# Products over 64 channels run over all 128 partitions, with zeros in the other half

## The chip, the cores and the metric

The kernel runs on one core of one Trainium2 chip. Times are device microseconds of one execution; the metric is their median over runs. The profile is that of one execution. PE is TensorE's matmul, PEld its weight load, DVE is VectorE, ACT is ScalarE, POOL is GpSimd and SP is SyncE, whose queue issues most of the DMAs.

## What is computed

Two transformer blocks on 512 tokens with 1024 features, all in float32. The first block has two groups of heads side by side, then a dense feed-forward part. The second has retention heads and differential attention heads, then a layer that picks neurons out of 16384 by product keys. The change touches the scores of three of these groups, all of them sums over 64 channels:

```python
# recurrent heads (mLSTM): q, k have 64 channels per head
jnp.einsum('bhctd,bhcsd->bhcts', qc, kc)
# latent heads: 128 channels without and 64 with rotary positions
k = jnp.concatenate([k_nope, k_pe], axis=-1)        # 128 + 64
s = jnp.einsum('bhqd,bhkd->bhqk', q_blk, kh) * scale
# differential heads: two score maps p per head, 64 channels each
s = jnp.einsum('bhpid,bhpjd->bhpij', qi, kt) + bias
```

## The kernel before

**Precision.** Most products are split in two parts. A float32 value x is kept as `hi`, a copy in the format fp32r, and `lo`, the rest x - hi. A product is then the sum of three fp32r matmuls (`mm3`, L130 to L132): hi by hi, hi by lo, lo by hi. Matmuls on plain float32 tiles are done by the hardware in two instructions each.

**Scores over 64 channels.** For the recurrent and the differential heads the three parts are packed. The first tile of a head has hi in one half of the 128 partitions and lo (or hi once more) in the other, so that one matmul over 128 partitions does two of the three parts. The third part, with the lo half alone, is a matmul over 64 partitions: L652 and L653 in `rec_weights` (tile pS), L837 and L838 in `dif_scores` (tile pDS). Which half of the partitions it uses goes with the head or with the map (`up` is partitions 0 to 63, `dn_` 64 to 127). For the latent heads (tile psc), L556 is the product over the 128 plain channels, and L557 the one over the 64 rotary channels; two heads lie in the two halves of qT1 and kT1.

**Stages.** The first block's input product gives the gates (F7), the latent inputs (ch, cl), the features of the recurrent heads (qk, ql, from tile pq and a convolution) and rows for v and the output gate (tile pts, `ts_mm`). From the gates a chain of scans makes UB (L394 to L398), which is transposed in four pieces (L543, tile pub) into the columns `cols` and `em`; the recurrent heads use them. `lat_in`, `lat_norm` and `lat_heads` make qT0, kT0, qT1 and kT1 per block of 128 tokens. The latent attention then runs over 16 pairs of a head and a block of queries, staged: scores of one pair, transposes (tile ppt, L572) of the pair before, product with v (tile pov, L582) of the one before that. The recurrent heads are staged alike: scores and weights (`rec_weights`, DVE's L664 and L668, ACT's L665 and L667), three steps later `rec_out` (tile pH). The differential heads too: `dif_scores`, `dif_turn` (pDT), `dif_out` (pD), with the features of later heads (tile pf) and products for later stages (pts) in between.

**What sets the order.** Each engine works through its own queue in order. The order in each queue is fixed when the program is compiled: a planner goes through the program by priority and by the costs that it expects, so that work of later stages (products pq, pts, pf) is placed in the gaps of earlier ones. Tiles live in pools; a tile with a tag and `bufs=n` shares n places, and the first write to a place waits until its former owner has been read for the last time. A pool that is opened where others have been closed waits in the same way. PSUM has eight banks, four of them ("att") for the tiles of the attention stages and four ("acc") for the longer sums.

Of the kernel before, what the change touches and what calls it, by code (L numbers as in the profile page):

```python
# [7 lines left out]
F32 = mybir.dt.float32  # L8
# [9 lines left out]
T = 512  # L18
D = 1024
P = 128  # L20
# [30 lines left out]
def body(ctx, tc, I, out):  # L51
# [17 lines left out]
    def bank(tag, name):  # L69
        p, n = banks[tag]  # L70
        return p.tile([P, 512], F32, tag=tag, name=name, bufs=n)
# [9 lines left out]
    V.memset(nhalf, -0.5)  # L81

    up, dn_ = slice(0, 64), slice(64, 128)

    def sub(eng, o, a, hi):
        eng.tensor_tensor(o, a, hi.bitcast(F32), op=OP.subtract)  # L86
# [157 lines left out]
    def out_last(x, w, h, l, spare, after):  # L244
        pg = []
        for half in range(2):
            for j in range(2):
                if half * j:
                    raw = fetch(w[4 * half + j])
                    for kk in range(2):  # L250
                        ph, pl = spare(), spare()
                        c = slice(kk * 512, (kk + 1) * 512)
                        S.activation(ph, raw[:, c], AF.Copy)
                        sub(V, pl, raw[:, c], ph)
                        pg.append((ph, pl))
                else:
                    wh, wl = page(w[4 * half + j])
                    pg += [(wh[:, kk * 512:(kk + 1) * 512], wl[:, kk * 512:(kk + 1) * 512]) for kk in range(2)]
        for tb in range(NT):
            t = slice(tb * P, (tb + 1) * P)  # L260
            for half in range(2):
                c = slice(half * 512, (half + 1) * 512)
                ps = bank("acc", "pol")
                for kt in range(4):
                    wh, wl = pg[4 * half + kt]
                    mm3(ps, h[:, kt, t], l[:, kt, t], wh, wl, kt == 0, kt == 3)
                V.tensor_tensor(x[tb][:, c], x[tb][:, c], ps, op=OP.add)
            after(tb)

# [47 lines left out]
    nc.sync.dma_start(gcq, I["g_c"])  # L317
    gq_b = bcast_row(I["g_q"], 192, "gq_b", m1)
    gk_b = bcast_row(I["g_k"], 192, "gk_b", m1)
    gm_b = bcast_row(I["g_mlstm_out"], 512, "gm_b", m1)  # L320
    sin = m1.tile([P, NT, 32], F32, name="sin")
    cos = m1.tile([P, NT, 32], F32, name="cos")
    kpe = m1.tile([P, NT, 4, 16], F32, name="kpe")
# [66 lines left out]
    Mx = F7[0:64]  # L390
    V.tensor_tensor_scan(Bc[0:4], zf[0:4], zero[0:4], 0.0, op0=OP.add, op1=OP.add)
    V.tensor_tensor_scan(Bc[32:36, ::-1], zf[32:36, ::-1], zero[32:36], 0.0, op0=OP.add, op1=OP.add)
    UB = mc.tile([P, T], F32, name="UB")
    G.memset(UB, 0.0)  # L394
    V.tensor_tensor(UB[0:R], F7[0:R], Bc, op=OP.subtract)
    V.tensor_tensor_scan(Mx[0:4], UB[0:4], UB[0:4], 0.0, op0=OP.max, op1=OP.max)
# [4 lines left out]
    sub(V, MxP[64:128], Mx, MxP[0:64])  # L401
    for d in range(2):
        V.tensor_tensor(sel[:, d], ident[:, 32 * d:32 * d + 4], ident[:, 64 + 32 * d:68 + 32 * d], op=OP.add)


    lp, lp_close = pool("latp")
# [30 lines left out]
    ukv = page(I["w_ukv"][0], into=hk)  # L437
    qT0 = [main.tile([P, 2, T], F32, tag="x", name="qT0", bufs=NT) for _ in range(2)]
    kT0 = [main.tile([P, 2, T], F32, tag="x", name="kT0", bufs=NT) for _ in range(2)]
    qT1 = mb.tile([P, 2, T], F32, name="qT1")  # L440
    kT1 = mb.tile([P, 2, T], F32, name="kT1")
    vv = mb.tile([P, NT, 512], F32, name="vv")

# [15 lines left out]
    for tb in range(NT):  # L459
        sq = lp.tile([P, 192], F32, tag="qsq", name="psq", bufs=1)  # L460
        S.activation(sq[:, 0:64], kflat[:, tb], AF.Square, accum_out=ssp[:, tb:tb + 1])
    kg = lp.tile([P, NT, 64], F32, name="kg")
    V.tensor_tensor(kg, kflat, gk_b[:, None, 128:192].to_broadcast([P, NT, 64]), op=OP.mult)
    kr = lp.tile([P, NT, 64], F32, name="kr")
    rope(kr, kg, cos, sin)
# [58 lines left out]

    def lat_heads(tb, key):
        nope, rot = lat[tb, key]
        T0, T1 = (kT0, kT1) if key else (qT0, qT1)
        t = slice(tb * P, (tb + 1) * P)
        pt = bank("att", "pqt")
        for hd in range(4):  # L530
            PE.transpose(pt[:, hd * P:(hd + 1) * P], nope[:, hd, :], ident)
        for j in range(2):
            S.activation(T0[j][:, :, t], pt[:, j * 256:(j + 1) * 256].rearrange("p (h t) -> p h t", h=2), AF.Copy)
        pt = bank("att", "pqt")
        for j in range(2):
            PE.transpose(pt[:, j * P:(j + 1) * P], rot[:, 2 * j:2 * j + 2, :].rearrange("p h d -> p (h d)"), ident)
        S.activation(T1[:, :, t], pt[:, 0:256].rearrange("p (h t) -> p h t", h=2), AF.Copy)

    staged([(tb, key) for tb in range(NT) for key in range(2)], lat_in, lat_norm, lat_heads)

    pt = bank("att", "pub")
    for tb in range(NT):
        PE.transpose(pt[:, tb * P:(tb + 1) * P], UB[:, tb * P:(tb + 1) * P], ident)  # L543
    S.activation(cols, pt.rearrange("p (t a b c) -> p t a b c", t=NT, a=2, b=2)[:, :, :, :, 0:4], AF.Copy)
    Ucol = cols[:, :, 0]
    S.activation(em, cols[:, :, 1], AF.Exp, scale=-1.0)

    ybh, ybl = [m1.tile([P, 4, T], F32R, tag="yb", name="yb", bufs=2) for _ in range(2)]
    att = {}

    def lat_scores(hd, qb):
        pp = slice(64 * (hd % 2), 64 * (hd % 2) + 64)
        j, jj = hd // 2, hd % 2
        q = slice(qb * P, (qb + 1) * P)
        ps = bank("att", "psc")
        PE.matmul(ps, qT0[j][:, jj, q], kT0[j][:, jj, :], start=True, stop=False)  # L556
        PE.matmul(ps, qT1[pp, j, q], kT1[pp, j, :], start=False, stop=True)  # L557
        mx = small(1, "mx")
        V.tensor_reduce(mx, ps, axis=AX.X, op=OP.max)
        V.tensor_scalar(mx, mx, rq[:, qb, hd:hd + 1], -1.0, op0=OP.mult, op1=OP.mult)  # L560
        pe_ = mb.tile([P, T], F32, tag="pe", name="pe", bufs=3)
        sm = small(1, "sm")
        S.activation(pe_, ps, AF.Exp, bias=mx, scale=rq[:, qb, hd:hd + 1], accum_out=sm)
        V.reciprocal(sm, sm)
        V.tensor_scalar(pe_, pe_, sm, None, op0=OP.mult)
        att[hd, qb] = pe_
# [25 lines left out]
    for i in range(4):  # L592
        ps = bank("acc", "pq")
        ws_mm(ps, page(wf[i]), h, l)
        cv = mc.tile([P, T], F32, tag="cv", name="cv", bufs=2)
        V.tensor_scalar(cv, ps, convw[:, i, 2:3], convw[:, i, 5:6], op0=OP.mult, op1=OP.add)
        for j in (0, 1, 3, 4):
            a, b = max(0, 2 - j), min(T, T + 2 - j)
            V.scalar_tensor_tensor(cv[:, a:b], ps[:, a + j - 2:b + j - 2], convw[:, i, j:j + 1], cv[:, a:b],
                                   op0=OP.mult, op1=OP.add)  # L600
        th = mc.tile([P, T], F32, tag="th", name="th", bufs=1)
        S.activation(th, cv, AF.Tanh, scale=0.5)
        V.scalar_tensor_tensor(th, th, 1.0, cv, op0=OP.add, op1=OP.mult)
        if i < 2:
            ql = mv.tile([P, T], F32R, name=f"ql{i}")
        for m, (own, other) in enumerate(((up, dn_), (dn_, up))):
            a = mv.tile([P, T], F32R, name=f"qk{i}{m}")
            S.activation(a[own], th[own], AF.Copy)
            if i < 2:
                S.activation(a[other], th[own], AF.Copy)  # L610
                sub(V, ql[own], th[own], a[own])
                qk.append((a, ql))
            else:
                sub(V, a[other], th[own], a[own])
                qk.append(a)
# [16 lines left out]

    ma, ma_close = pool("rec")
    og = ma.tile([P, NT, 512], F32, name="og")
    rec = {}

    def rec_max(hd):
# [7 lines left out]
    def rec_weights(hd, sb):  # L645
        if sb == 0:
            rec_max(hd)
        pp = (up, dn_)[hd % 2]
        (qh, ql), kk = qk[hd], qk[4 + hd]
        sps = bank("att", "pS")  # L650
        t = slice(sb * P, (sb + 1) * P)
        PE.matmul(sps, kk[:, t], qh, start=True, stop=False)  # L652
        PE.matmul(sps, kk[pp, t], ql[pp], start=False, stop=True)  # L653
        for d in range(2):
            mp = rec[hd][d]
            uc = Ucol[:, sb, d, hd:hd + 1]
# [40 lines left out]
    for tb in range(NT):  # L697
        load_x(x, tb)
    out_half(x, I["w_out"], ybh, ybl, range(4), 2)
    yh, yl = [ma.tile([P, 4, T], F32R, name=n) for n in ("yh", "yl")]  # L700
    for hd in range(4):
        hs, hss = rec[hd, "o"]
        rh = small(4, "rh")
# [3 lines left out]
        for tb in range(NT):  # L707
            V.scalar_tensor_tensor(ya[:, tb], hs[:, tb], rh[:, tb:tb + 1], og[:, tb, hd * 128:(hd + 1) * 128],
                                   op0=OP.mult, op1=OP.mult)
            PE.transpose(pt[:, tb * P:(tb + 1) * P], ya[:, tb], ident)  # L710
        S.activation(yh[:, hd, :], pt, AF.Copy)
        sub(V, yl[:, hd, :], pt, yh[:, hd, :])
    h, l, _, norm, norm_end = norm_T(x, "g_ffn_norm")
    out_last(x, I["w_out"], yh, yl, lambda: ma.tile([P, T], F32R, tag=f"E{T}", name="X", bufs=4), norm)
    ma_close()
# [84 lines left out]

    def dif_key(hd, ps):
        B = [md.tile([P, T], F32R, tag=f"dk{m}", name="dk", bufs=2) for m in range(2)]
        kl = md.tile([P, T], F32R, tag="dkl", name="dkl", bufs=2)
        for m, (own, other) in enumerate(((up, dn_), (dn_, up))):
            S.activation(B[m][own], ps[own], AF.Copy)
            S.activation(B[m][other], ps[own], AF.Copy)
            sub(V, kl[own], ps[own], B[m][own])
        feat["k", hd] = B, kl

    def dif_head(hd):  # L810
# [16 lines left out]
    def dif_scores(hd, qb):  # L827
# [4 lines left out]
        w = max(n, 256)  # L832
        (B, kl), A = feat["k", hd], feat["q", hd]
        es, sms = [], []
        for m, pp in enumerate((up, dn_)):
            ps = bank("att", "pDS")
            PE.matmul(ps[:, 0:w], A[m][:, q], B[m][:, 0:w], start=True, stop=False)  # L837
            PE.matmul(ps[:, 0:w], A[m][pp, q], kl[pp, 0:w], start=False, stop=True)  # L838
            e = md.tile([P, T], F32, tag="sv", name="sv", bufs=5)
            V.scalar_tensor_tensor(e[:, 0:n], tri[:, T - n:T], float(2.0 ** (-8.0 * (hd + 1) / 4)), ps[:, 0:n],  # L840
                                   op0=OP.mult, op1=OP.add)
# [116 lines left out]

    staged([(hd, b) for hd in range(4) for b in range(NT)], ret_weights, skip, skip, skip, ret_out, *[skip] * 4, ret_norm)
    h, l, rows, norm, norm_end = norm_T(x, "norm_ffn_g")  # L960
    out_last(x, I["w_out2"], yh, yl, lambda: ma.tile([P, T], F32R, tag="X", name="X", bufs=4), norm)
    xn3 = rows[3]
    ma_close()
    mr_close()
# [477 lines left out]
```

## Time and profile before

| | |
|---|---|
| median of 3 runs | 2127.32 us (2127.05 to 2130.56) |
| profiled execution | 2128.51 us, span of its instructions 2126.7 us |
| mean granted TensorE clock | 0.995 |
| PE busy | 2090.7 us, 98% of the span |
| DVE busy | 1541.3 us, 72% |
| ACT busy | 858.6 us, 40% |
| POOL busy | 534.6 us, 25% |
| latent scores, first to last | 116 to 170 us |
| recurrent scores | 175 to 218 us |
| differential scores | 666 to 794 us |

The first row is what the change is timed by. The durations of single instructions come from the profiled execution, whose own time is the second row; its span runs from the first to the last instruction. Busy times of PE are of pipelined matmuls: the time between the starts of two neighbours says more than the length of one.

### The profile page before, as it was taken

What the parts mean: (1) busy time and instruction counts of PE and PEld (TensorE: products, weight loads), DVE (VectorE), ACT (ScalarE), POOL (GpSimd) and SP (SyncE); (2) the same over time, 40 slices, a digit from 0 to 9 for tenths busy, and PEclk for the clock granted to TensorE, in tenths of its full rate; (3) what the DMA queues carried; (4) which work ended last, traced back from release to release, by engine and by line L of the source; (5) the groups of instructions that cost most, each with busy time, mean ns of one, the idle gap of its engine ahead of it and who ended that gap; (6) DMA issues with size and microseconds to landing.
All of it is one profiled execution on the core that took longest, in us unless ns stands there. A gap on an engine that the chain in (4) does not pass through costs nothing.

```text
span 2126.7 us, 29751 instructions
## 1 busy us (share of the span) xinstructions
PE 2090.7 (98%) x10985; PEld 1807.7 (85%) x10985; DVE 1541.3 (72%) x3039; ACT 858.6 (40%) x1505; POOL 534.6 (25%) x387
## 2 busy tenths in 40 slices
PE   7999999999999999999999999999999999999998
PEld 6856888888888778888999999999888889899886
DVE  6846666556444763679979799978888878778784
ACT  5645354444324543311335544333333333333332
POOL 1100034444100000100000004544555554444330
PEclk9999999999999999999999999999999999999999
DMA  5210269899512222354898778999999999998981
GB/s 191 68 41 21 90 239 353 318 340 345 205 60 89 69 70 91 108 199 165 278 352 302 280 228 312 372 360 338 319 343 333 351 319 338 330 335 319 322 291 61
DMA packets 178977, 507.55 MB, mean 239 GB/s; under 512 B 15632, under 2 KB 73872, under 8 KB 172048
## 3 DMA queue, kind: packets, MB, share of 16 engines
q1 hardware_dynamic: 136208, 329.47, 45.6%
q0 software_dynamic: 42624, 176.18, 22.0%
q8 instruction: 86, 1.41, 0.3%
q14 instruction: 59, 0.48, 0.1%
HBM read 428.52 MB, written 77.07 MB: 238 GB/s over the span
## 4 chain that ended last, share of the span: by engine, by line
PE 96%; DVE 1%; DMA 1%; ACT 1%; issue 0%; SPq 0%; POOL 0%; DVEq 0%; POOLq 0%; ACTq 0%
PE pA L130 11%; PE pA L131 11%; PE pA L132 11%; PE po L132 8%; PE po L130 8%; PE po L131 8%; PE pO L131 3%; PE pO L132 3%; PE pO L130 3%; PE pts L132 2%; PE pts L130 2%; PE pts L131 2%; PE pGm L1147 2%; PE pQ L130 1%; PE pQ L131 1%; PE pQ L132 1%
## 5 line engine op out<-in xcount | busy, mean ns | idle before, releaser
L130 PE MATMUL pA<-xTh,Ah 128*128 128x384 f32 (+1 forms) x1256 | 434.0, 346 | 0.3 <-ACT ge L1166 0.3
L132 PE MATMUL pA<-xTh,Al 128*128 128x384 f32 (+1 forms) x1256 | 434.2, 346 | 0.0
L131 PE MATMUL pA<-xTl,Ah 128*128 128x384 f32 (+1 forms) x1256 | 434.0, 346 | 0.0
L105 ACT ACTIVATE Ah<-raw 128x1024 fp32r<-128x1024 f32 x203 | 215.1, 1060 | 329.9 <-PE pA L131 228.2
L86 DVE TENSOR_TENSOR Al<-raw,Ah 128x1024 fp32r<-128x1024 f32 x202 | 249.8, 1237 | 122.7 <-ACT Ah L105 119.1
L1236 POOL DMA_INDIRECT gu<-peer_u_rows,eidx x128 | 182.6, 1426 | 581.0 <-issue 394.3
L132 PE MATMUL po<-Bh,Wl 128*128 128x512 f32 x714 | 278.6, 390 | 0.0
L131 PE MATMUL po<-Bl,Wh 128*128 128x512 f32 x714 | 278.2, 390 | 0.0
L131 PEld LDWEIGHTS pA<-xTl,Ah 128*128 128x128 f32 x1256 | 235.9, 188 | 14.3
L130 PEld LDWEIGHTS pA<-xTh,Ah 128*128 128x128 f32 x1256 | 235.8, 188 | 14.1 <-ACT ge L1166 0.6
L132 PEld LDWEIGHTS pA<-xTh,Al 128*128 128x128 f32 x1256 | 235.8, 188 | 12.0
L1236 POOL DMA_INDIRECT gv<-peer_v,eidx x128 | 190.2, 1486 | 197.2 <-DVE acc L1252 180.2
L130 PE MATMUL po<-Bh,Wh 128*128 128x512 f32 x714 | 225.0, 390 | 0.0
L86 DVE TENSOR_TENSOR Bl<-raw,Bh 128x1024 fp32r<-128x1024 f32 x151 | 193.7, 1284 | 19.9 <-ACT Bh L105 19.2
L1297 ACT ACTIVATE Wh<-w 128x384 fp32r<-128x384 f32 x128 | 67.1, 525 | 342.8 <-PE po L131 313.1
L105 ACT ACTIVATE Bh<-raw 128x1024 fp32r<-128x1024 f32 x151 | 157.7, 1049 | 68.2 <-PE pO L132 45.9
L1252 DVE SCALAR_TENSOR_TENSOR acc<-gv,w,acc 128x1024 f32<-128x1024 f32 x128 | 164.0, 1281 | 2.2 <-DMA gv<-peer_v,eidx 2.2
L1242 DVE SCALAR_TENSOR_TENSOR gu<-gu,hn 128x1024 f32<-128x1024 f32 x128 | 155.8, 1219 | 3.8 <-DMA gu<-peer_u_rows,eidx 3.8
L132 PEld LDWEIGHTS po<-Bh,Wl 128*128 128x128 f32 x714 | 134.0, 188 | 26.2
L86 DVE TENSOR_TENSOR Wl<-w,Wh 128x384 fp32r<-128x384 f32 x128 | 71.1, 556 | 117.4 <-ACT Wh L1297 109.5
L131 PEld LDWEIGHTS po<-Bl,Wh 128*128 128x128 f32 x714 | 134.1, 188 | 25.7
L130 PEld LDWEIGHTS po<-Bh,Wh 128*128 128x128 f32 x714 | 133.2, 188 | 22.1
(410 smaller groups left out, 3778.6 us busy)
## 6 DMA issues: line engine op xcount, KB each, us to landing
raw<-peer_v SPq DMA_DIRECT2D x128, 512.0 KB, 6.4
raw<-peer_u SPq DMA_DIRECT2D x104, 512.0 KB, 6.5
Sd<-shl POOLq DMA_DIRECT2D x40, 1024.0 KB, 7.8
raw<-w_ff SPq DMA_DIRECT2D x64, 512.0 KB, 6.2
Gd<-stage SPq DMA_DIRECT2D x12, 2048.0 KB, 7.5
Gt<-Gd SPq DMA_DIRECT2D x32, 768.0 KB, 7.5
Al<-Sd SPq DMA_DIRECT2D x40, 512.0 KB, 5.9
Ah<-Sd SPq DMA_DIRECT2D x40, 512.0 KB, 5.5
```

Of the source, the lines that this page charges most:

```text
L86: eng.tensor_tensor(o, a, hi.bitcast(F32), op=OP.subtract)
L105: S.activation(hi, raw, AF.Copy)
L130: PE.matmul(ps, lh, rh, start=start, stop=False)
L131: PE.matmul(ps, lh, rl, start=False, stop=False)
L132: return PE.matmul(ps, ll, rh, start=False, stop=stop)
L1147: PE.matmul(o, hot[:, 0, jp, :, jb], val[:, p, jp, :, jb], start=p == 0, stop=p == 1)
L1236: G.indirect_dma_start(out=r, out_offset=None, in_=rows, in_offset=bass.IndirectOffsetOnAxis(ap=eidx[s // 64][:, s % 64:s % 64 + 1], axis=0))
L1242: V.scalar_tensor_tensor(r, r, 1.0, xn3, op0=OP.mult, op1=OP.mult, accum_out=act3[:, s:s + 1])
L1252: V.scalar_tensor_tensor(acc3, r, w3[:, s:s + 1], acc3, op0=OP.mult, op1=OP.add)
L1297: S.activation(wh, w, AF.Copy)
```

## The change

All three products now run over 128 partitions. The half of the small operand that doesn't belong to the product is filled with zeros (`half_tile`, a fill by POOL); the other operand is used whole. qT1 and the differential kl and recurrent ql become two tiles, one for either half. To make room, UB and one half of qT1 share a place (tag q1), the other half of qT1 shares the place of the norm gain row (tag gb), the recurrent features become one tag (qk, 8 places) that yh and yl take over later, kg shares a place with ra, and gm_b is loaded into the later pool `rec`. Since UB's place is given on, its transposes and the copies to `cols` and `em` move from behind `lat_heads` to just behind the scans. The evacuation of the latent queries becomes two ACT instructions of 64 partitions each.

```diff
+    def half_tile(pool, shape, dt, other, **kw):
+        t = pool.tile(shape, dt, **kw)
+        z = t[other]
+        G.memset(z.bitcast(F32) if dt == F32R else z, 0.0)
+        return t
...
-    gm_b = bcast_row(I["g_mlstm_out"], 512, "gm_b", m1)
...
-    UB = mc.tile([P, T], F32, name="UB")
+    UB = mb.tile([P, 2, T], F32, tag="q1", name="UB", bufs=1)[:, 0]
...
+    pt = bank("att", "pub")
+    for tb in range(NT):
+        PE.transpose(pt[:, tb * P:(tb + 1) * P], UB[:, tb * P:(tb + 1) * P], ident)
+    S.activation(cols, pt.rearrange("p (t a b c) -> p t a b c", t=NT, a=2, b=2)[:, :, :, :, 0:4], AF.Copy)
+    Ucol = cols[:, :, 0]
+    S.activation(em, cols[:, :, 1], AF.Exp, scale=-1.0)
...
-    qT1 = mb.tile([P, 2, T], F32, name="qT1")
+    qT1 = [half_tile(p, [P, 2, T], F32, o, tag=t, name="qT1", bufs=1)
+           for p, t, o in ((mb, "q1", dn_), (main, "gb", up))]
...
-    kg = lp.tile([P, NT, 64], F32, name="kg")
+    kg = lp.tile([P, NT, 64], F32, tag="ra", name="kg", bufs=1)
...
-        S.activation(T1[:, :, t], pt[:, 0:256].rearrange("p (h t) -> p h t", h=2), AF.Copy)
+        for dst, own in (((kT1, slice(0, P)),) if key else ((qT1[0], up), (qT1[1], dn_))):
+            S.activation(dst[own, :, t], pt[own, 0:256].rearrange("p (h t) -> p h t", h=2), AF.Copy)
...
-        PE.matmul(ps, qT1[pp, j, q], kT1[pp, j, :], start=False, stop=True)
+        PE.matmul(ps, qT1[jj][:, j, q], kT1[:, j, :], start=False, stop=True)
...
-            ql = mv.tile([P, T], F32R, name=f"ql{i}")
-            a = mv.tile([P, T], F32R, name=f"qk{i}{m}")
+            a = mv.tile([P, T], F32R, tag="qk", name="qk", bufs=8)
+            if i < 2:
+                ql = half_tile(mv, [P, T], F32R, other, name=f"ql{i}{m}")
...
+    gm_b = bcast_row(I["g_mlstm_out"], 512, "gm_b", ma)
...
-        PE.matmul(sps, kk[pp, t], ql[pp], start=False, stop=True)
+        PE.matmul(sps, kk[:, t], ql, start=False, stop=True)
...
-    yh, yl = [ma.tile([P, 4, T], F32R, name=n) for n in ("yh", "yl")]
+    yh, yl = [[mv.tile([P, T], F32R, tag="qk", name=n, bufs=8) for _ in range(4)] for n in ("yh", "yl")]
...
-        kl = md.tile([P, T], F32R, tag="dkl", name="dkl", bufs=2)
+        kl = [half_tile(md, [P, T], F32R, o, tag=f"dkl{m}", name="dkl", bufs=2) for m, o in enumerate((dn_, up))]
...
-            PE.matmul(ps[:, 0:w], A[m][pp, q], kl[pp, 0:w], start=False, stop=True)
+            PE.matmul(ps[:, 0:w], A[m][:, q], kl[m][:, 0:w], start=False, stop=True)
```

## Rows read from the trace of the kernel before

**Rows 1.** The page: busy time by engine; the chain that ended last.
```profile
PE 2090.7 (98%) x10985; PEld 1807.7 (85%) x10985; DVE 1541.3 (72%) x3039; ACT 858.6 (40%) x1505; POOL 534.6 (25%) x387
...
PE 96%; DVE 1%; DMA 1%; ACT 1%; issue 0%; SPq 0%; POOL 0%; DVEq 0%; POOLq 0%; ACTq 0%
```
**Rows 2.** Busy time of each engine by stretch: PE, PEld, DVE, ACT, POOL.
```profile
60.00:116.00 56.00, 54.57 (x271) 45.85 (x271) 44.99 (x107) 42.23 (x115) 10.06 (x9) 1.00 0.20 66
...
180.00:195.00 15.00, 13.99 (x81) 10.05 (x81) 14.55 (x62) 12.58 (x46) 0.86 (x1) 1.00 0.01 2
195.00:222.00 27.00, 27.00 (x145) 21.21 (x144) 14.92 (x57) 11.00 (x39) 2.16 (x3) 1.00 0.07 20
660.00:800.00 140.00, 140.00 (x643) 109.23 (x642) 87.27 (x213) 74.14 (x175) 3.03 (x3) 1.00 0.25 80
```
**Rows 3.** Lines L557, L653, L838: ns min/median/max, first and last start, forms.
```profile
L557 PE MATMUL psc<-kT,qT x32: 589/589/693, 118.4 to 169.6; 64*128 64x512 f32 x32
...
L653 PE MATMUL pS<-ql,qk x16: 491/497/502, 175.7 to 217.4; 64*128 64x512 f32 x16
...
L838 PE MATMUL pDS<-dkl,dq x32: 378/412/502, 666.8 to 793.9; 64*128 64x256 f32 x16, 64*128 64x384 f32 x8, 64*128 64x512 f32 x8
```
**Rows 4.** Latent stage in time: start us, length us, instruction, [idle before].
```profile
130.68 0.30 PEld L556 LDWEIGHTS psc<-kT,qT 128*128 128x128 f32 x2
130.78 1.02 PE L556 MATMUL psc<-kT,qT 128*128 128x512 f32 x2
...
131.74 0.29 PEld L557 LDWEIGHTS psc<-kT,qT 64*128 64x128 f32 x2 [0.76 <-issue]
131.74 1.12 PE L557 MATMUL psc<-kT,qT 64*128 64x512 f32 x2
131.74 0.49 DVE L565 TENSOR_SCALAR pe<-pe,sm 128x512 f32<-128x512 f32 x1
...
132.79 0.42 PEld L572 LDWEIGHTS ppt<-ident,pe 128*128 128x128 f32 x4 [0.76 <-issue]
132.79 0.66 PE L572 MATMUL ppt<-ident,pe 128*128 128x128 f32 x4
```
**Rows 5.** Recurrent stage, PE in time, with filler products around one score.
```profile
199.55 0.40 PE L131 MATMUL pts<-Al,xTh 128*128 128x512 f32 x1
199.78 0.40 PE L652 MATMUL pS<-qk,qk 128*128 128x512 f32 x1
200.11 0.50 PE L653 MATMUL pS<-ql,qk 64*128 64x512 f32 x1
200.54 0.50 PE L132 MATMUL pts<-Ah,xTl 128*128 128x512 f32 x1
200.88 0.40 PE L130 MATMUL pts<-Ah,xTh 128*128 128x512 f32 x1
```
**Rows 6.** Differential stage, PE in time, around one score of 256 columns.
```profile
711.34 0.27 PE L837 MATMUL pDS<-dk,dq 128*128 128x256 f32 x1
711.55 0.38 PE L838 MATMUL pDS<-dkl,dq 64*128 64x256 f32 x1
711.86 0.51 PE L131 MATMUL pf<-xTl,Ah 128*128 128x512 f32 x1
712.20 0.28 PE L837 MATMUL pDS<-dk,dq 128*128 128x256 f32 x1
```
**Rows 7.** Tile UB: its transposes and its last write.
```profile
L543 PE MATMUL pub<-ident,UB x4: 272/272/273, 116.0 to 116.3; 128*128 128x128 f32 x4
...
L398 DVE TENSOR_TENSOR UB<-Bc,F x1: 686/686/686, 53.1 to 53.1; 36x512 f32<-36x512 f32 x1
```
**Rows 8.** Tile qT: the evacuation of the rotary part of the queries.
```profile
L537 ACT ACTIVATE qT<-pqt x4: 377/385/462, 74.9 to 114.9; 128x256 f32<-128x256 f32 x4
```
**Rows 9.** POOL by line and form: the largest fill.
```profile
L394 POOL MEMSET UB<- 128x512 f32 x1 | 0.5, 521 | 0.0
```
**Rows 10.** Tile gm_b: its only readers.
```profile
L626 DVE SCALAR_TENSOR_TENSOR og<-og,gm_b x4: 689/690/694, 231.2 to 235.2; 128x512 f32<-128x512 f32 x4
```

## What the change should do to the time

> **What bounds the kernel.** I read the page first: TensorE (PE) is busy 98% of the span and the chain that ended last is 96% PE [rows 1], so time is won only where PE's queue gets shorter and nothing else is waited for. Next came the stretches in which the touched products run [rows 2]. From 195 to 222 us and from 660 to 800 us PE is busy all the time, with DVE at 55 to 62% and ACT at 41 to 53%: PE sets the pace there. From 180 to 195 us DVE is busy 14.55 of 15 us and PE has holes: DVE sets the pace there, and a shorter PE queue buys nothing. From 60 to 116 us PE leads again (54.57 of 56). Then the views by line give the counts [rows 3]: the 64-row products are 32 instructions on L557 (a product of plain fp32 takes two, so 16 products), 16 on L653 and 32 on L838. Last, the instructions in order of time show what one such product costs.
>
> Look at the latent scores first [rows 4]. The load for L556 starts at 130.68, while the matmul before it still runs, and the two L556 matmuls are 0.43 us apart (1.02 of the pair less 0.59 of the last one, the 0.59 being the usual length in rows 3 for L557 too). Before L557, PEld stands idle 0.76 us and the 64-row load starts only with its own matmul, at 131.74; the step from the second L556 (131.21) to it is 0.53. Inside the L557 pair the step is 0.53 again, since the first matmul had to wait for its load, and out of it, 132.27 to 132.79, 0.52. The load of the following 128-row transpose is again not ahead (0.76 idle). So 128-row work before and after a 64-row product loses the overlap of load and matmul on both sides.
>
> **What one switch costs.** Latent, fp32: three steps of 0.52 to 0.53 where 0.43 would do, 0.29; and the four transposes behind it take (0.66 - 0.27)/3 = 0.13 a step instead of 0.11 [rows 4, 7], 0.05 in all. Together 0.34 us a product. Recurrent, fp32r, 512 wide [rows 5]: an undisturbed step is 0.23; from L652 to the second matmul of the filler behind L653 there are three steps, 199.78 to 200.88, 1.10 us where 3 x 0.23 = 0.69 would do: 0.41, I use 0.40. Differential, 256 wide [rows 6]: 711.34 to 712.20 is 0.86 for two steps of half width and one of full width; 0.12 + 0.12 + 0.23 = 0.47 would do: 0.39. The price does not depend on the width, so it is the switch and not the streaming; I use 0.39 for all 32.
>
> **What the change does to it.** All three products now have 128 rows, like their neighbours. No trace shows these with zeros in half the rows; the nearest rows are the 128-row products next to them, which stream at 0.23 (512 wide, fp32r) and 0.43 (fp32). From below, a 128-row product costs no less than those steps; from above, it costs what the 64-row one does now. I take the lower end, since rows 4 to 6 show the very same operands (kk, dq, kT0) at it. If everything were paid out: 16 x 0.34 + 16 x 0.40 + 32 x 0.39 = 5.4 + 6.4 + 12.5 = 24.3 us.
>
> A page of the Trainium skill speaks against this. "TensorE: Matmul & The Clock Gate", Part 3, "What overlaps and what doesn't", says that a weight load overlaps running matmuls only if it goes to other row groups. By that, loads for all 128 rows could never be hidden, the change would win nothing, and the sum would stay at 2127.7; by the rows it is 2108.3. The trace doesn't agree with it: the 128-row L556 load runs under the matmul before it [rows 4], and 512-wide steps of 0.23 leave no room for a load of 0.18 to 0.19 that is not hidden. I keep a small chance for its outcome.
>
> **What of the 24.3 us reaches the end.** Latent: the softmax of one block must be ready when PE comes to its transposes. DVE's L565 ends at 132.23 and the transposes start at 132.79 [rows 4], 0.56 of slack. With the change PE comes by 0.34 earlier in each period, and the scores end only 0.09 less before the transposes; at worst 0.43 of the slack goes, 0.13 stays. So PE remains the limit there. The first two blocks run before the pipeline is full and then wait for the first softmax; I count them half: 15 x 0.34 = 5.1. Recurrent: ten of the 16 products lie before 195 us, where DVE sets the pace [rows 2]; I count those as nothing and the six behind 195 in full: 6 x 0.40 = 2.4. Differential: filler products of other heads stand between, DVE and ACT are idle 38 to 47% of the stretch; I count 32 x 0.39 = 12.5 less 0.6, my allowance for single copies that come just in time: 11.9.
>
> **The other edits.** The four UB transposes (L543) move from 116 us to just behind the gate scans. They are 0.11 us each [rows 7], 0.44 in all. From one side, they filled an idle moment of PE at 116 and now take the time of other products: 0.44 lost; from the other, they now fill one of the holes of the early stretch: 0.44 won. I take 0.4 lost, since PE is nearly full in the new place [rows 2]. They can't run before UB is complete, 53.1 + 0.7 = 53.8 [rows 7]; PE issues in order, so if they are queued too early PE stands. UB is needed 21 us before its slot gets its new owner qT1, so there is room; a wait is a rival below. The two small ACT copies (cols, em) go along. The latent query evacuation of 128 partitions becomes two of 64: four more ACT instructions of at most 0.46 each [rows 8], 1.8 us at most, hidden in ACT's 14 us of idle time between 60 and 116 [rows 2]; without that cover 1.8 would be the price. Twelve zero fills of 64x512 and two of 64x1024 are added on POOL: the nearest row, 128x512, is 0.52 [rows 9], so about 12 x 0.52 + 2 x 1.04 = 8.3 us, on an engine that is busy 3.03 of 140 us in the differential stretch and 10.06 of 56 in the latent one [rows 2]. POOL's other work there is the small power operations behind the norms; behind a fill one of these could be late by 0.5 to 1 us, and PE has other products to issue meanwhile. DVE's work is unchanged in count and width. kg moving into ra's slot, yh and yl in the slots of qk, and UB in a slot with qT1 wait for nothing that is not long done in program order: nothing. Two DMAs move: gm_b leaves the start and is loaded into a pool that opens after the latent stage; it is first read at 231.2 [rows 10]. The g_ffn_norm row shares its slot with half of qT1 now, so it can be loaded only after the last L557 (169.6, rows 3), and is read only after og is used; both have tens of us of cover on SP's queue: nothing.
>
> **Sum.** 5.1 + 2.4 + 11.9 - 0.4 = 19.0 us. The profiled execution took 2128.51 us (span 2126.7 and 1.8 around it), 1.2 above the median of the three runs, 2127.32. 2128.5 - 19.0 = 2109.5 for such an execution, 2127.3 - 19.0 = 2108.3 as a median.
>
> **The rivals.** (A) As summed, 2108.3, own range 2104 to 2113: 0.60. (B) The DVE-paced recurrent stretch pays too, because its first work starts earlier or the order of the filler changes, and the 1.0 us of PE holes there [rows 2] close: up to 24.3 + 1.0, 2102 to 2104. For it: its scores are ready earlier; against: DVE 14.55 of 15. 0.12. (C) New waits eat part: PE order was fixed for the old steps, and with the latent slack down to 0.13 and ready-just-in-time copies in the differential stage, half of the latent term (2.5), a third of the differential one (4) and a PE wait for UB of up to 5 us would go: 2112 to 2120. For it: one in-order queue; against: the slack found. 0.15. (D) The loss isn't tied to rows, or full loads do not overlap: the steps stay, 0.4 is added: 2127.7. Against: every step of 128-row work in rows 4 to 6. 0.07. (E) Slower: gm_b lands late. Its place is free only when the latent stage has ended, and SP issues in order; if SP stands before it behind loads that wait for slots, DVE's L626 waits, the accumulator banks stay full and PE stops. Each us behind 231.2 is a us; it decides from a landing at 231.2 + 19 = 250 us on, and at 255 gives 2132. Against: 60 us between the last latent product (169.6, rows 3) and 231. 0.06.
>
> About 0.2% (4 us) is what a measurement of this kernel can tell from no change. A, B and C are faster by more than that (0.87), D is within it (0.07), E is slower (0.06). The range reaches over A and most of B and C, 2100 to 2119; D and E stay out.
>
> **What would show it.** Right: no 64-row form is left; PE's step L556 to L557 is 0.43, L652 to L653 and on to the filler 0.23, L837 to L838 at 256 wide about 0.12; PEld shows no idle time of 0.2 to 0.8 us put down to issue at these lines. The latent period shrinks by 0.34; 180 to 195 stays DVE-bound, with more holes in PE; everything behind 800 us comes some 19 us earlier, unchanged in itself. Wrong: steps of 0.4 between 128-row fp32r products (D); PE waiting at L543 for UB or at L572 for DVE's L565 (C); DVE's L626 waiting for gm_b (E); or a span behind 800 us that itself changes in length, since that part is untouched by this argument.

## The result and the profile after

The changed kernel took 2109.39 us as the median of 6 runs (2107.54 to 2112.2), the kernel before, run beside it, 2125.78 (2121.5 to 2130.56). The ratio is 0.9928, 95% interval 0.9916 to 0.9939: faster by 13 to 18 us. Predicted were 2108.3 and a gain of 19.0.

First the page of the changed kernel, busy time by engine and the chain that ended last, which answer to [rows 1].

```profile
PE 2068.0 (98%) x10985; PEld 1808.5 (86%) x10985; DVE 1538.2 (73%) x3039; ACT 858.5 (41%) x1509; POOL 542.6 (26%) x401
...
PE 86%; DVE 6%; DMA 4%; issue 2%; ACT 1%; POOL 0%; SPq 0%; DVEq 0%; POOLq 0%; ACTq 0%
```

PE does as many instructions as before and is busy 22.7 us less. It is still the engine that sets the end; that its share of the chain is 86% and not 96% comes from the part behind 1196 us, where the chain now goes over loads and DVE as well; that part is as long as before to within 1 us. POOL has 14 instructions and 8.0 us more: the zero fills. The same stretches as in [rows 2], with the same columns:

```profile
60.00:116.00 56.00, 50.26 (x247) 42.04 (x246) 40.21 (x99) 41.04 (x117) 9.57 (x8) 0.95 0.21 66
180.00:195.00 15.00, 13.72 (x82) 11.47 (x81) 12.35 (x58) 11.01 (x44) 1.01 (x1) 1.00 0.00 1
195.00:222.00 27.00, 27.00 (x166) 23.95 (x165) 16.48 (x67) 13.21 (x43) 2.53 (x3) 1.00 0.14 40
660.00:800.00 140.00, 140.00 (x703) 118.10 (x702) 84.94 (x213) 75.62 (x183) 6.12 (x8) 1.00 0.27 81
```

In the 140 us of the differential stretch PE now gets through 703 matmuls where it did 643. The recurrent stage comes 4.9 us earlier than before, so 180 to 195 us is not the same piece of it; from 175 to 190 us DVE is busy 14.50 of 15 us and PE 13.45, so DVE still sets the pace there. In the stretch from 60 to 116 us, ahead of the latent scores, PE has lost 4.3 us of work and its granted clock is 0.95 on the mean: something went wrong there. Now the three lines, by form, with shortest, median and longest ns, as in [rows 3]; no 64-row form is left.

```profile
L564 PE MATMUL psc<-kT,qT x32: 592/592/1061, 119.1 to 164.8; 128*128 128x512 f32 x32
...
L660 PE MATMUL pS<-ql,qk x16: 389/396/401, 170.7 to 209.3; 128*128 128x512 f32 x16
...
L845 PE MATMUL pDS<-dkl,dq x32: 277/308/397, 658.0 to 772.9; 128*128 128x256 f32 x16, 128*128 128x384 f32 x8, 128*128 128x512 f32 x8
```

In order of time, first a latent period (to be read against [rows 4]), then a recurrent score [rows 5], then a differential one of 256 columns [rows 6]:

```profile
130.01 1.02 PE L563 MATMUL psc<-kT,qT 128*128 128x512 f32 x2
130.44 0.19 PEld L564 LDWEIGHTS psc<-kT,qT 128*128 128x128 f32 x1 [0.24 <-issue]
130.87 1.02 PE L564 MATMUL psc<-kT,qT 128*128 128x512 f32 x2
...
131.73 0.60 PE L579 MATMUL ppt<-ident,pe 128*128 128x128 f32 x4
...
133.06 0.59 PE L563 MATMUL psc<-kT,qT 128*128 128x512 f32 x1
...
198.06 0.47 PE L659 MATMUL pS<-qk 128*128 128x512 f32 x1
198.37 0.40 PE L660 MATMUL pS<-ql,qk 128*128 128x512 f32 x1
198.60 0.40 PE L138 MATMUL pts<-Al,xTh 128*128 128x512 f32 x1
...
708.83 0.19 PEld L845 LDWEIGHTS pDS<-dkl,dq 128*128 128x128 f32 x1
708.95 0.28 PE L845 MATMUL pDS<-dkl,dq 128*128 128x256 f32 x1
708.95 0.19 PEld L138 LDWEIGHTS pf<-xTl,Ah 128*128 128x128 f32 x1
...
709.06 0.39 PE L138 MATMUL pf<-xTl,Ah 128*128 128x512 f32 x1
```

Latent: from the first L563 to the first L564 are 0.86 us for two steps, on to the transposes 0.86 again, and the period is 133.06 - 130.01 = 3.05 where it was 3.39. Recurrent: the step behind L660 is 0.23; the 0.31 ahead of it is that of a first wide product behind the short ones of pH, and where L659 follows a wide product it is 0.22 to 0.24. Differential: 0.11 from L845 to the filler. The load for L138 takes from 708.95 to 709.14, while L845's matmul (708.95 to 709.23) runs: loads for 128 rows overlap.

The last group belongs to the stretch before the latent scores: PE in order of time around the early transposes (against L543 in [rows 7]) and just ahead of the scores.

```profile
49.52 0.39 PE L137 MATMUL pq<-xTh,Ah 128*128 128x512 f32 x1
50.29 0.66 PE L413 MATMUL pub<-ident,UB 128*128 128x128 f32 x4 [0.39 <-DVE UB L404]
50.78 2.74 PE L439 MATMUL prc<-ones,csq 128*128 128x1 f32 x24
53.38 0.42 PE L137 MATMUL puq<-wu,ch 128*128 128x384 f32 x1
...
105.68 0.39 PE L139 MATMUL puq<-hk,cl 128*128 128x512 f32 x1
105.91 0.60 PE L545 MATMUL pqt<-ident,na 128*128 128x128 f32 x4
106.26 0.72 PE L649 MATMUL pM<-MxP,sel 128*128 128x512 f32 x2
106.84 0.44 PE L550 MATMUL pqt<-ident,ro 128*128 128x128 f32 x2
107.90 0.66 PE L545 MATMUL pqt<-ident,na 128*128 128x128 f32 x4 [0.62 <-ACT vv L496]
108.45 0.44 PE L550 MATMUL pqt<-ident,ro 128*128 128x128 f32 x2
113.96 1.09 PE L545 MATMUL pqt<-ident,na 128*128 128x128 f32 x4 [5.08 <-DVE na L523]
```

Behind the last puq at 105.68, PE has only transposes and pM left, and then stands 5.08 us until DVE has the last normalised keys. The granted clock from 112 to 120 is 0.50, the lower level (1.2 of 2.4 GHz), and behind the first latent matmul the next four steps are 0.85 us each and not 0.43.

Where each stage starts, profile against profile: the first latent score is 0.9 us earlier, the first recurrent one 4.9, the last recurrent one 8.1, the first product of the feed-forward part 8.7, the end of the differential stage 21.3, and the end of the span 20.8. What lies behind 812 us changed by 0.5 us in itself. The 20.8 is more than the runs give, since the profiled execution before was 2.7 us above the median of the runs beside the change, the one after 1.7 below its own. In the one before, PE also lost some us between 44 and 56 us (granted clock 0.72). Two experiments whose early part is the same program (the first two below) came to the first latent score at 110.9 and 110.2 us, not at 116.5; so the -0.9 hides a loss.

### The profile page after: what moved, and what is told of

Same layout as the page of the kernel before. It is cut to its first block, busy times and chain, and to the rows that moved or that the text cites. A ratio compares the mean times of both kernels' runs of the same rounds, so it can differ in the third digit from the quotient of the medians.

```text
span 2105.9 us, 29794 instructions
## 1 busy us (share of the span) xinstructions
PE 2068.0 (98%) x10985; PEld 1808.5 (86%) x10985; DVE 1538.2 (73%) x3039; ACT 858.5 (41%) x1509; POOL 542.6 (26%) x401
## 4 chain that ended last, share of the span: by engine, by line
PE 86%; DVE 6%; DMA 4%; issue 2%; ACT 1%; POOL 0%; SPq 0%; DVEq 0%; POOLq 0%; ACTq 0%
PE pA L137 9%; PE pA L138 9%; PE pA L139 9%; PE po L137 7%; PE po L139 7%; PE po L138 7%; PE pO L138 3%; PE pO L139 3%; PE pO L137 3%; PE pts L138 2%; PE pts L137 2%; PE pts L139 2%; PE pGm L1154 2%; DMA raw<-peer_v 2%; PE pQ L137 1%
## 5 line engine op out<-in xcount | busy, mean ns | idle before, releaser
L138 PE MATMUL pA<-xTl,Ah 128*128 128x384 f32 (+1 forms) x1256 | 434.2, 346 | 0.0
L138 PE MATMUL po<-Bl,Wh 128*128 128x512 f32 x714 | 278.4, 390 | 0.0
L138 PEld LDWEIGHTS pA<-xTl,Ah 128*128 128x128 f32 x1256 | 235.9, 188 | 14.2
L138 PEld LDWEIGHTS po<-Bl,Wh 128*128 128x128 f32 x714 | 134.1, 188 | 25.6
```

Of the source, the lines that this page charges most:

```text
L138: PE.matmul(ps, lh, rl, start=False, stop=False)
```

## The experiments

Twelve kernels, each timed in five rounds; ratios are to the kernel before, run beside them. "Late" is UB's old place behind `lat_heads`, "early" is that of the change.

### Is it the switch, and what does it cost in each stage?

**Grouped.** The kernel before, differential stage alone: the two 128-row products of a block first, then its two 64-row products, so half as many switches.

```diff
+        pss = [bank("att", "pDS") for _ in range(2)]
+        for m in range(2):
+            PE.matmul(pss[m][:, 0:w], A[m][:, q], B[m][:, 0:w], start=True, stop=False)
...
         for m, pp in enumerate((up, dn_)):
+            PE.matmul(pss[m][:, 0:w], A[m][pp, q], kl[pp, 0:w], start=False, stop=True)
```

> The kernel before, with one edit: in each block of the differential scores both 128-row products are issued first and both 64-row products after them. The number of rows stays as it was. Theory 1 (the loss is the switch between row counts): 64 single 64-row products in 32 pairs of switches become 16 pairs, 16 x 0.39 = 6.2 us less if going from the lower to the upper half is no switch of its own, 3 us less if it is. Theory 2 (a 64-row product costs 0.39 us by itself, whatever stands beside it): the same time as before, within 1 us.

2120.78 us, ratio 0.9979 (0.997 to 0.9988), 5.5 us less by the medians (2.6 to 6.4 by the interval). In the trace the differential stage took 3.7 us less, of which 3.0 reach the end. Not all the pairs stayed together in the order written at compile time, only 7 of 16, so 7 x 0.39 = 2.7 us are what theory 1 gives for this order. PE in order of time, at such a pair:

```profile
682.17 0.38 PE L839 MATMUL pDS<-dkl,dq 64*128 64x256 f32 x1
682.49 0.50 PE L837 MATMUL pDS<-dk,dq 128*128 128x256 f32 x2
682.92 0.39 PE L839 MATMUL pDS<-dkl,dq 64*128 64x256 f32 x2
683.24 0.50 PE L130 MATMUL pf<-xTh,Ah 128*128 128x512 f32 x1
```

The single L839 at 682.17 is followed after 0.32 us. The pair at 682.92 takes 0.39 for both: the raw records start 4 ns apart, the two products using opposite halves. The pair costs 0.32 us to the next product, as much as the single one. A cost of each 64-row product by itself would have left the time unchanged, unless two that run side by side share it. The latent rows speak against that: the two L557 matmuls of a score [rows 4] run one behind the other in the same half, and together cost 0.34, no more than a single product here. So the price goes with the switch.

**Differential part alone.** The kernel before with only `kl` as two zero-filled tiles and L838 over 128 rows:

```diff
-            PE.matmul(ps[:, 0:w], A[m][pp, q], kl[pp, 0:w], start=False, stop=True)
+            PE.matmul(ps[:, 0:w], A[m][:, q], kl[m][:, 0:w], start=False, stop=True)
```

> The kernel before with the differential part of the change alone (two kl tiles with zeros). Theory 1: 32 x 0.39 = 12.5 us less in a stretch where PE sets the pace, and nothing lost behind it: 12 to 12.5 us less in the end, ratio 0.994; nothing changes ahead of 660 us. Rival (the gain is given back by the stages behind, which wait for transfers or DVE): less than 9 us in the end, with new PE gaps behind 800 us.

2114.22 us, ratio 0.9943 (0.9929 to 0.9956), 12.1 us by the medians. In the trace, the first feed-forward product comes 7.6 us earlier than in the profile before, the last differential output 20.1, everything behind by as much: the stage itself gives 12.5. That is the whole price of 32 x 0.39.

**Latent part alone.** Only qT1 as two tiles and L557 over 128 rows; UB keeps a place of its own and is transposed late.

```diff
-        PE.matmul(ps, qT1[pp, j, q], kT1[pp, j, :], start=False, stop=True)
+        PE.matmul(ps, qT1[jj][:, j, q], kT1[:, j, :], start=False, stop=True)
```

> The kernel before with the latent part of the change alone (two qT1 tiles with zeros, the second in the place of the norm gain row); UB keeps its own place, and its transposes stay behind the latent heads. Theory 1: the period of a block falls from 3.39 to 3.05 us, 14 or 15 x 0.34 = about 5 us less. Theory 3 (the gap of 5.08 us before the first latent score of the changed kernel and the half clock behind it come from the moved edits: the UB transposes, gm_b, kg): no such gap here, PE waits at most 1.5 us near 115 us and the first scores run at full clock, as before the change. Rival (they come from the doubled query evacuation on ACT): the gap stands here too, and the gain shrinks to 1 or 2 us.

2118.35 us, ratio 0.9957 (0.9943 to 0.9971): 6 to 12 us, where about 5 were expected. The period is 3.05, as in the full change. There is no gap of 5 us ahead of the scores: the longest is 0.86, and the clock of the first scores is 1.00.

**The moves alone.** UB early and in one place with qT1, gm_b late, kg in ra's place; all products keep 64 rows. The pub block of six lines moves as in the change, and:

```diff
-    UB = mc.tile([P, T], F32, name="UB")
+    UB = mb.tile([P, 2, T], F32, tag="q1", name="UB", bufs=1)[:, 0]
...
-    qT1 = mb.tile([P, 2, T], F32, name="qT1")
+    qT1 = mb.tile([P, 2, T], F32, tag="q1", name="qT1", bufs=1)
```

> The kernel before with the moved edits alone: UB in the place of qT1 and its transposes early, gm_b loaded into the later pool, kg in the place of ra. All products keep 64 rows. Theory 3: the early stretch runs ahead by about 8 us up to 72 us (no PE wait at 47 us, no half clock behind it), then the filler is used up before the latent heads are ready, a gap of about 5 us stands at 114 us and the first scores run at half clock; in the end within 2 us of before. Rival: the early stretch is as before the change, and these edits cost the 0.4 us of the prediction.

2131.75 us, ratio 1.003 (1.002 to 1.004): the moves cost 5.5 us, more than either theory said. The early transposes stand 1.33 us waiting for UB, but PE also has a gap of 4.6 us at 115.5, and the clock is down behind it.

**The moves with late transposes.** The same, but the pub block behind `lat_heads` and UB in a place of tag PT:

```diff
-    UB = mc.tile([P, T], F32, name="UB")
+    UB = mb.tile([P, T], F32, tag="PT", name="UB", bufs=2)
```

> The kernel before with gm_b in the later pool, kg in the place of ra and UB in a place of tag PT; the UB transposes stay where they were and all products keep 64 rows. Theory 4: within 1 us of before (the 5.5 us that all moved edits together cost come from the transposes alone). Rival (gm_b's load or kg's place delay the latent heads): 3 to 5 us more than before.

2125.91 us, ratio 1.0005 (0.9995 to 1.0016): nothing. So gm_b and kg cost nothing, as forecast, and the early pub block does.

**The recurrent part, with these moves.** The kernel just told, with `ql` as zero-filled tiles and:

```diff
-        PE.matmul(sps, kk[pp, t], ql[pp], start=False, stop=True)
+        PE.matmul(sps, kk[:, t], ql, start=False, stop=True)
```

> The kernel before with the recurrent part of the change alone (four ql tiles with zeros, yh and yl in the features' places) and, to make room, gm_b, kg and UB placed as in the run before. Theory of the prediction (from 175 to 195 us DVE sets the pace, six of 16 products count): 2.4 us less than before. Rival (PE sets the pace in all of it): 6.4 us less.

2122.34 us, ratio 0.999 (0.998 to 1.0001), 2.5 us by the medians, forecast 2.4. The interval leaves out the 6.4 of the rival, but not a gain of nothing, so the trace must say more. Against the trace of the moves with late transposes, the recurrent stage alone is 3.1 us shorter, some 8 switches of 0.40 out of 16.

### What in the early transposes costs so much?

**The change with late transposes.** All else as in the change:

```diff
-    UB = mb.tile([P, 2, T], F32, tag="q1", name="UB", bufs=1)[:, 0]
+    UB = mb.tile([P, T], F32, tag="PT", name="UB", bufs=2)
...
-    pt = bank("att", "pub")
...
     staged([(tb, key) for tb in range(NT) for key in range(2)], lat_in, lat_norm, lat_heads)
+    pt = bank("att", "pub")
...
```

> The changed kernel with the UB transposes, cols and em put back behind the latent heads; UB lies in a place of tag PT then, not in qT1's. Theory 4 (in the changed kernel the four transposes at 50.3 us stand ahead of the first latent input products in PE's queue and start the chain of the latent heads 5 us late): the first product puq starts before 46 us again instead of at 53.4, the first latent score near 110 us at full clock, no gap over 2 us there, and the time is 5 us below that of the changed kernel, ratio 0.990. Rival (the doubled query evacuation or the zero fills slow the latent heads): gap and time as in the changed kernel, 0.993.

2102.17 us, ratio 0.9894 (0.9876 to 0.9912): faster than both kernels, and 7.2 us below the changed one, where 5 were forecast. The first puq starts at 44.25 us, the first latent score at 113.23 at full clock, and the longest gap ahead of it is 0.85 us: as theory 4 forecast but for the first score, which it put at 110.

**Half-way.** The pub block just ahead of the staged latent heads; UB still shares its place with qT1.

```diff
+    pt = bank("att", "pub")
...
     staged([(tb, key) for tb in range(NT) for key in range(2)], lat_in, lat_norm, lat_heads)
```

> The changed kernel with the UB transposes, cols and em moved to just ahead of the latent heads' loop; UB and qT1 still share a place. Theory 4: the order in PE's queue is what counts, so puq starts early and the time is as in the run before, 0.990. Rival (the shared place counts: the first half tile can be filled and written only when UB has been read): a wait of the latent heads on POOL or ACT and a time between 0.990 and 0.993.

2102.14 us, ratio 0.9893 (0.9876 to 0.991). The shared place costs nothing. But theory 4 fails in its mechanism: the first puq does not start early here, it starts at 53.60 us, as late as in the changed kernel (53.38), and nothing is lost by it.

**The exponential late.** The change, with only this line behind the latent heads again:

```diff
-    S.activation(em, cols[:, :, 1], AF.Exp, scale=-1.0)
...
     staged([(tb, key) for tb in range(NT) for key in range(2)], lat_in, lat_norm, lat_heads)
+    S.activation(em, cols[:, :, 1], AF.Exp, scale=-1.0)
```

> The changed kernel with one line moved back: the exponential of em runs behind the latent head block again, while the four UB transposes and the copy to cols stay early. Theory 1 (the early transposes themselves cost about 7 us: PE works in order, and the first products of the latent projections, puq, stand behind them until UB is complete): puq still starts at about 53 us, PE still has a gap of about 5 us near 114, and the time stays that of the changed kernel, about 2109.4. Theory 2 (ACT's part costs it: the exponential brings a table load of 1.28 us at 51 us and holds up the copies of the latent inputs behind it): the time falls to about 2102 to 2104, and the gap near 114 shrinks below 2 us.

2109.05 us, ratio 0.9918 (0.9903 to 0.9932). Theory 1 as expected; ACT's table load is not it.

**Transposes that wait for nothing.** The early pub block reads the identity and not UB:

```diff
-        PE.transpose(pt[:, tb * P:(tb + 1) * P], UB[:, tb * P:(tb + 1) * P], ident)
+        PE.transpose(pt[:, tb * P:(tb + 1) * P], ident, ident)
```

> The changed kernel, but the four early transposes read the identity matrix and not UB, so they have nothing late to wait for; the columns cols and em hold other values, all else is as in the changed kernel, the table load of em included. Theory 1 (the cost comes from UB's late end, about 50 us, and what stands behind it in PE's queue): prc and the first puq start at 43 to 45 us again, the gap near 114 is below 2 us, the granted clock there stays 1.00 or falls only briefly, and the time is 2101 to 2104. Theory 2 (four transposes, a copy and an exponential in the early stretch cost by their mere presence there): the time stays at about 2109.

2109.16 us, ratio 0.9922 (0.9908 to 0.9937). My theory 1 fell. pub runs at 35.7 us, prc and the first puq are back at 42.33 and 43.14, and yet:

```profile
42.33 0.95 PE L439 MATMUL prc<-ones,csq 128*128 128x1 f32 x8
43.14 0.42 PE L137 MATMUL puq<-wu,ch 128*128 128x384 f32 x1
...
105.87 0.39 PE L139 MATMUL puq<-hk,cl 128*128 128x512 f32 x1
106.10 0.60 PE L545 MATMUL pqt<-ident,na 128*128 128x128 f32 x4
106.45 1.18 PE L649 MATMUL pM<-MxP,sel 128*128 128x512 f32 x4
...
114.05 1.09 PE L545 MATMUL pqt<-ident,na 128*128 128x128 f32 x4 [5.07 <-DVE na L523]
```

The early part is as it was, the end is that of the change: no pts behind the last puq, then the same gap. In all kernels PE does the same 548 matmul instructions ahead of the scores; what differs is how many filler products the written order leaves for the end. So theory 3: the order at the end of the stretch is the cost. Seen on ACT in the changed kernel, in order of time, the squares of the last key block (qsq, L509), from which its norm comes, stand between copies for earlier blocks:

```profile
106.81 0.37 ACT L509 ACTIVATE qsq<-puq,rkv 128x128 f32<-128x128 f32 x1
...
107.17 0.68 ACT L496 ACTIVATE vv<-puq,rkv 128x512 f32<-128x512 f32 x1
...
109.74 0.78 ACT L552 ACTIVATE qT<-pqt 64x256 f32<-64x256 f32 x2
110.54 0.37 ACT L509 ACTIVATE qsq<-puq,rkv 128x128 f32<-128x128 f32 x1
```

The fourth square ends at 110.9, the power on POOL and DVE's product follow, and the transposes wait until 113.96.

**Behind prc.** The early pub block moved back by some fifteen lines, to just behind the loop of prc:

```diff
             PE.matmul(pr[:, 4 * i + tb:4 * i + tb + 1], sqs[i][:, tb * P:(tb + 1) * P], ones, start=True, stop=True)
+    pt = bank("att", "pub")
...
     ssc = lp.tile([P, 8], F32, name="ssc")
```

> The changed kernel with the UB block moved back by some fifteen lines, from just ahead of the twelve small products prc (two instructions each) to just behind them. In the order written out at compile time, nine of the filler products pts then stand behind the last puq products; in the changed kernel, and in the kernel whose early transposes read the identity, none does. Theory 3 (the loss is that filler is used up before the last latent blocks are normalised, so PE stands idle for 5 us and its clock falls behind that): the gap near 112 us is below 2 us, the granted clock from 112 to 120 stays mostly at 1.00, the time is 2101 to 2104. Theory 4 (transposes and copies anywhere in the early stretch cost it): 2107 to 2110.

2102.02 us, ratio 0.9891 (0.9874 to 0.9908), as theory 3 expects. PE's order at the end, in time:

```profile
104.07 0.40 PE L139 MATMUL puq<-hk,cl 128*128 128x512 f32 x1
104.30 0.40 PE L139 MATMUL pts<-Ah,xTl 128*128 128x512 f32 x1
...
106.38 0.39 PE L137 MATMUL puq<-hk,ch 128*128 128x512 f32 x1
...
106.85 0.40 PE L139 MATMUL puq<-hk,cl 128*128 128x512 f32 x1
...
110.39 0.66 PE L543 MATMUL pqt<-ident,na 128*128 128x128 f32 x4 [0.68 <-DVE na L521]
```

The nine pts stand between the two halves of the last puq block (the expectation put them behind it; behind it is one). The squares of the first half are so done while PE works, the fourth ends at 107.4 and not at 110.9, and the gap is 0.68. By the windows, the granted clock from 112 to 120 is 1.00, in the changed kernel 0.50. The first puq is at 53.36 us here too.

The other traces agree. In the five kernels that have no pts behind the last puq (the change, the moves alone, the exponential late, the identity, the acc bank) PE stands 4.2 to 5.1 us ahead of these last transposes; in the other nine, with 1 to 11 pts behind it, 0.7 to 1.4. The chain itself differs too: from the last puq to these transposes are 5.5 us in the kernel before, 8.3 in the changed one and 3.5 with the block behind prc. So the written order is shown as the cause; how much of the gap is missing filler on PE and how much the place of the squares on ACT is not separated.

**Another bank.** The early pub block in an acc bank:

```diff
-    pt = bank("att", "pub")
+    pt = bank("acc", "pub")
```

> The changed kernel with the early UB transposes in one of the four acc banks of PSUM and not in an att bank. In the order written out at compile time, no filler product pts stands behind the last two blocks of puq products, which is one block earlier than in the changed kernel. Theory 3 (order of the filler): a gap of PE of 5 us or more remains between 108 and 118 us, perhaps with a second one ahead of it, and the time is 2109 to 2115. Theory 5 (an att bank given to pub early delays the next tiles of the att ring, prc and the first transposes pqt): the gap falls below 2 us and the time is 2101 to 2104.

2118.09 us, ratio 0.9968 (0.9956 to 0.998), slower than either theory said. PE in time:

```profile
41.22 1.86 PE L439 MATMUL prc<-ones,csq 128*128 128x1 f32 x8 [5.52 <-ACT csq L433]
...
124.79 1.09 PE L545 MATMUL pqt<-ident,na 128*128 128x128 f32 x4 [4.18 <-DVE na L523]
```

The gap at the end is there, with the clock at 0.54 from 124 to 128 us; theory 5 is out. The rest are new waits, 5.52 us at 41 us and 2.00 for UB at 49.4, which come with the acc bank: this run changed two things, and its total tells nothing more.

## Why the prediction was right, and where it was not

The gain was right within 3 us, and part of that is luck: two errors offset each other. The place of the pub block cost 6 to 7 us where 0.4 was forecast, and the padded products, timed one part at a time, gave 22.6 where 19.4 was forecast.

- **Switch cost.** Right in size, and in cause as far as the grouped run and the padded ones show it. The steps are 0.43, 0.23 and 0.12 as forecast, and no 64-row form is left. Rival D is out. The Trainium skill's rule that a load overlaps only with work on other row groups ("TensorE: Matmul & The Clock Gate", Part 3, "What overlaps and what doesn't") doesn't hold for these 128-row products: steps of 0.12 us are shorter than the loads of 0.19 between them.
- **Differential, 11.9.** Measured 12.5 in the stage (timed 12.1). My allowance of 0.6 for copies that come just in time was not needed; rival C's third of this term didn't go.
- **Recurrent, 2.4.** Measured 2.5 timed, 2.7 to 3.3 in the traces. DVE still sets the pace in the first part of the stage, and PE has holes there, the longest 0.91 us, waiting for weights E; rival B is out.
- **Latent, 5.1.** Right in the stage. From the first latent score to the first recurrent one are 57.55 us in three kernels with 64-row products (grouped, differential part, recurrent part) and 52.55 to 52.57 in four with padded ones (latent part, late transposes, half-way, behind prc), all at full clock: 5.0 us, of which 13 steady periods of 0.344 less make 4.5. Between the two kernels with late transposes the stage differs by 6.3 us, but 1.3 of this is clock: behind a wait of 1.89 us for the first softmax the granted clock was 0.57 from 118 to 122 us in the moves with late transposes, and 1.00 in the change. It was 1.00 in the run of the recurrent part too, whose latent products still have 64 rows; so I don't count it to the change. What the timed latent part gives above 5.0 (8.0 by the medians, 6 to 12 by the interval) lies outside the stage and stays open.
- **The moved transposes, 0.4.** The step that failed. I priced the four transposes by their own length and asked whether they would wait. I called PE nearly full in their new place by [rows 2], but those rows begin at 60 us and the place is at 50. They wait 0.39 us; the block costs 5.5 with the products unchanged and 7.2 in the full change. I didn't ask what its place does to everything behind it in the written order: 3.3 to 3.6 us are lost up to the first latent score (115.52 us against 112.18 half-way and 111.94 behind prc), and 2.3 in the latent stage, in steps at half clock. Rival C named a wait for UB of up to 5 us: the size was about right, the mechanism was not, since the cost stays where nothing is waited for, and goes away with the block behind prc.
- **The other edits, nothing.** Right: moves with late transposes, 1.0005. gm_b is issued at 170.81 and lands 3.0 us later, long before its first reader:

```profile
L633 DVE SCALAR_TENSOR_TENSOR og<-og,gm_b x4: 686/690/694, 223.0 to 227.0; 128x512 f32<-128x512 f32 x4
```

  Rival E didn't come; [rows 10] had the reader at 231.2. The zero fills are 14 on POOL, and no engine waits for them.
- **By parts.** 12.1 + 8.0 + 2.5 = 22.6 us by the medians of the parts, 22.7 for the change with late transposes. The change as made gives 16.4, so some 6.3 are lost to the place of the pub block (7.2 by the two times themselves; the runs of the kernel before beside them differ by 0.95).

Open: why the planner, with pub ahead of prc, spends the filler sooner. The traces show the order it wrote, not its reasons.

## What to carry over

Where a 64-row contraction stands between full ones on PE, filling it with zeros to all 128 rows paid here 0.34 to 0.40 us a product, as long as PE sets the pace; read the steps around it, not the lengths. When an edit moves instructions to make room, cost the order behind them as well as their wait: look how much filler is left for the end of the stretch, where the last chain of norm and transposes has nothing to hide under, and what the other engines have queued ahead of that chain. Time such a move by itself; here a block moved back by fifteen lines gave 7 us more than the change as made.

## What the runs showed of the hardware

Two 64-row products on opposite halves of the partitions, one behind the other, start 4 ns apart and run side by side; at 256 columns the pair costs 0.32 us, a single one as much. Padded, the two cost 0.24, two steps of 0.12, and need no pairing. The granted clock behind one and the same wait differs: behind the 1.89 us for the first softmax it was 0.63 from 122 to 126 us in the kernel before, part of it at the lower level (1.2 of 2.4 GHz), and stayed at 1.00 in the grouped kernel and in that of the differential part alone, whose program is the same up to there. This moves a profile by some 1.3 us with no edit behind it. Over whole executions it is more: those of the kernel before with a mean granted clock of 0.994 took 2127.4 us on the mean (13 executions), those with 0.998 took 2121.1 (4).
